# A one-column exp behind the last Silu of the seven-product stage

## The chip, the cores and the metric

The kernel runs on one core of a Trainium2 chip. The metric is the device time of one execution in microseconds (us). The core has five instruction streams that matter here: TensorE (PE, with its weight loads shown apart as PEld), VectorE (DVE), ScalarE (ACT), GpSimd (POOL) and the sync engine (SP), which only issues transfers (DMA). Each stream runs its own instructions in order and waits on semaphores for the others. ACT evaluates functions such as exp and Silu from a table that has to be loaded first: the program shows such a load as `ACT_TABLE_LOAD`, and the compiler puts one in wherever the next function is not in the table that stands loaded.

## The reference, cut to what matters

The reference is one layer of an encoder with two branches over 1024 positions and 16 learned leading ones:

```python
z = rms_norm(h, pre_w) @ w_in                       # one projection for everything
rq, rk, rv, rg, aq, ak, av, ag, gr, ga = split(z)
# branch A: bidirectional retention over chunks of 128, group norm, times silu(rg)
y_r = (norm(retention(rq, rk, rv)) * silu(rg)) @ w_rb
# branch B: attention in a window of +-128 with a sink logit per head
s = where(ok, (q @ k.T) * scale, -1e30)             # and 16 keys that are always seen
m = maximum(max(s), sink); p = exp(s - m)
p = p / (sum(p) + exp(sink - m))
y_a = (p @ v * silu(ag)) @ w_ab
out = h + rms_norm((sigmoid(gr) * y_r + sigmoid(ga) * y_a) @ w_o, post_w)
```

## The kernel before

All products are made in float32 from pairs of rounded halves: `mm3` (L92 to L97) issues three matmuls for each, high times high, low times high and high times low, and so L94, L95 and L96 carry nearly all of PE's time. The large projections are done by a scheme with seven block products in place of eight (`Phase`). The stage that the change speaks of is the first such phase, `first_phase`, which makes the gates `rg` (units 0 to 3, names that end in `y`) and the queries of the attention. Its epilogue for a gate tile is `z_post` (L1318): a multiply by the row norm on DVE (L1321), a Silu on ACT (L1331), a multiply by the retention's output on DVE (L1334), and a store (L1335). Behind it comes `attention()`.

The attention walks over 32 blocks of 64 queries by 4 heads. For a block, `stage1` makes the scores `ps` on PE, adds the mask and takes the row minimum `nm` on DVE (L1525, into one `raw` tile for each of two halves), takes exp on ACT (L1528, tile `p`, with the row sums `den`), the reciprocal of the sums on DVE (L1531) and the scaling of `p` on POOL (L1538). `stage2` transposes `p` on PE into `pt` (L1549, L1552) and splits it in halves on ACT (`pah`, `pbh`, L1555 and L1556) and DVE (`pal`, `pbl`, L110). `stage3` multiplies by the values (`vah`, `val`, and a small tile `v` for the edges) into `po`. Between these steps `fill` puts pieces of later projections (`pe`, whose copy out of PSUM is L886 and whose store is L887; `we` are their weights, loaded at L854 and summed on DVE at L861 to L863) as work for PE.

The order within each stream is set when the program is recorded, by a scheduler that orders instructions by a simulated timeline. `follow(...)` (L99) ties what is recorded inside it to come after given instructions; `marks(...)` looks the given names up in `last`, where lines such as L1528 (`last["exp"] = ...`) keep the newest instruction of a kind.

Transfers from SP go in turn over eight lanes, `DMAHW0` to `DMAHW7`: each waits until the one before it on its lane, eight rows ahead, has landed.

Of the kernel before, what the change touches and what calls it, by code (L numbers as in the profile page):

```python
# [7 lines left out]
F32 = mybir.dt.float32  # L8
R = mybir.dt.float32r
AF = mybir.ActivationFunctionType  # L10
# [6 lines left out]
P = 128  # L17
# [38 lines left out]
def block_kernel(ctx: ExitStack, tc: tile.TileContext, xT, x, meta, w_in, w_rb, w_ab, w_out, vecs, dec, sink,  # L56
                 post_w, rope, tab, out):
    nc = tc.nc
    PSUM = bass.MemoryType.PSUM

    keep = ctx.enter_context(tc.tile_pool(name="keep", bufs=1))
# [37 lines left out]
    def follow(*ins):  # L99

        st = ExitStack()
        for i in ins:
            st.enter_context(tc.issue_after(i))
        return st
# [11 lines left out]
    dtab = keep.tile([P, 28], F32, name="dtab")  # L116
    rcol = keep.tile([P, 9], F32, name="rcol")
    rbc = keep.tile([P, T], F32, name="rbc")
    rnw = keep.tile([P, KT], F32, name="rnw")
    mhalf = keep.tile([P, 16], F32, name="mhalf")  # L120
    nc.vector.memset(mhalf, -0.5)
# [802 lines left out]
    softmax, last = [], {}  # L924

    def marks(*names):
        return [last[m] for m in names if m in last]
# [383 lines left out]
    def z_fetch(u, i, j):  # L1311
        if u < 8:
            d = (oTr_d if u < 4 else oTa_d)[2 * (u % 4) + i, :, 512 * j:512 * j + 512]
            v = gtile(f"v{u}{i}{j}")
            nc.sync.dma_start(v, d)
            fetched[u, i, j] = v, d

    def z_post(u, i, j, o, to=None):  # L1318
        s = slice(512 * j, 512 * j + 512)
        to = o if to is None else to  # L1320
        nc.vector.tensor_tensor(to, o, rbc[:, half[j]], mul)  # L1321
        while late:
            late.pop()()
        if u >= 8:
            nc.scalar.activation(to, to, AF.Tanh, scale=0.5)
            nc.sync.dma_start(tg_d[2 * (u - 8) + i, :, s], to)
            return
        if u in (0, 1):
            z_fetch(u, i, j)
        v, d = fetched.pop((u, i, j))  # L1330
        nc.scalar.activation(to, to, AF.Silu)  # L1331

        def gated():
            nc.vector.tensor_tensor(to, to, v, mul)  # L1334
            nc.sync.dma_start(d, to)  # L1335
        late.append(gated)
# [118 lines left out]
    def first_post(u, i, j, o, to=None):  # L1455
        (query_post if u > 15 else z_post)(u - 16 * (u > 15), i, j, o, to)

    def first_fetch(u, i, j):
        if 1 < u < 16:
# [5 lines left out]
    first_seq[-14:] = [(u, p) for p in (1, 5, 6, 7, 4, 2, 3) for u in FIRST[-2:]]  # L1465
    first_phase = Phase("y", first_seq, w_loader(w_in, gates), first_post, first_fetch, paired=True)
    steps = run([(Phase("z", sequence(EARLY + LATER, (1, 3, 2, 5, 6, 7, 4)), pre_loader, z_post, z_fetch,
                        early=EARLY, pre=PRE),
                  act_src(oTr_d)),
# [260 lines left out]
        do(table, n)  # L1730
    zq_stack.close()
    gates_[0] = 6
    free[:] = ["pj"] * 3
    e_from[0] = pj
    a_stack = ExitStack()
# [147 lines left out]
```

## Time and profile before

| | us |
|---|---|
| three runs, median | 1052.22 |
| three runs, lowest and highest | 1050.63, 1053.98 |
| the profiled execution's own time | 1050.95 |
| its span in the trace | 1049.1 |
| PE busy in the span | 1029.7 |
| ACT busy in the span | 510.5 |

The profile shows one execution. Its times run from the start of the span; the 1.85 us between the span and the execution's own time lie around it. In the timeline a row gives the start, the duration, the engine, the line of the kernel, the operation, and out<-in; what stands in brackets is the idle time of the engine just before, and what ended it. `SPq` rows are transfers being issued, not their duration. In the chain of waits a DMA row runs from the issue to the landing.

### The profile page before, as it was taken

The page shows a single profiled execution, that of the slowest core. Times are in us where ns is not written, and L with a number is a line of the kernel's source. Part 1 is how long each engine was busy: PE and PEld are TensorE (multiplying, and loading weights), DVE is VectorE, ACT ScalarE, POOL GpSimd, SP SyncE. Part 2 cuts the span into 40 slices and gives each one's busy share as a digit, 9 for nine tenths or more (in the row PEclk, how much of TensorE's full clock was granted, in tenths as well). Part 3 has the DMA queues.
Part 4 walks back from the last instruction along what each step waited for, and adds up shares of the span by engine and source line. Part 5 has one row for each costly group of instructions (what it writes and reads, how often), then busy time and mean ns, then how long its engine had stood idle before and what let it go on. Part 6 is the DMA issues. An engine that isn't in the chain of part 4 may idle for free.

```text
span 1049.1 us, 17233 instructions
## 1 busy us (share of the span) xinstructions
PE 1029.7 (98%) x5797; PEld 892.3 (85%) x5797; DVE 841.5 (80%) x1734; ACT 510.5 (49%) x1116; POOL 216.5 (21%) x284
## 2 busy tenths in 40 slices
PE   9999999999999999999799999999999999999997
PEld 8998999989999888888689998888888888787885
DVE  7887788779899787985867886699899799767665
ACT  5541441423445643424567776476567354343443
POOL 3424235234232002231123331000000000111042
PEclk9999999999999999999899999999999999999999
DMA  9322311315244499998867784999899638789365
GB/s 340 157 81 91 102 42 51 112 38 194 78 145 139 137 413 311 264 308 217 310 212 218 240 250 154 359 383 337 307 301 334 233 130 276 195 243 305 94 101 81
DMA packets 117577, 217.17 MB, mean 207 GB/s; under 512 B 12672, under 2 KB 44320, under 8 KB 114864
## 3 DMA queue, kind: packets, MB, share of 16 engines
q1 hardware_dynamic: 110896, 204.52, 56.6%
q0 software_dynamic: 6304, 11.01, 7.3%
q8 instruction: 46, 0.75, 0.3%
q10 hardware_dynamic: 288, 0.53, 0.2%
q14 instruction: 43, 0.35, 0.1%
HBM read 142.57 MB, written 77.12 MB: 209 GB/s over the span
## 4 chain that ended last, share of the span: by engine, by line
PE 84%; DVE 6%; DMA 6%; issue 1%; POOL 1%; SPq 1%; ACT 1%; DVEq 0%; POOLq 0%; ACTq 0%
PE bz L95 5%; PE bz L94 5%; PE bz L96 5%; PE by L95 4%; PE by L94 4%; PE by L96 4%; PE pv L95 3%; PE pv L96 3%; PE pv L94 3%; PE bo L95 3%; PE bo L94 3%; PE br L95 2%; PE bo L96 2%; PE br L94 2%; PE br L96 2%; PE ba L95 2%
## 5 line engine op out<-in xcount | busy, mean ns | idle before, releaser
L94 PE MATMUL pv<-wh,big 128*128 128x256 f32 x256 | 73.3, 286 | 0.0
L95 PE MATMUL pv<-wh,big 128*128 128x256 f32 x256 | 72.9, 285 | 0.0
L96 PE MATMUL pv<-wl,big 128*128 128x256 f32 x256 | 72.5, 283 | 0.0
L1538 POOL TENSOR_SCALAR p<-p,den 128x352 f32<-128x352 f32 (+2 forms) x60 | 38.2, 650 | 125.6 <-DVE den L1531 100.3
L1369 POOL DMA_DIRECT2D mx_d<-c1a x4 | 3.5, 873 | 287.3 <-DVE c1a L1360 287.3
L94 PE MATMUL bz<-T,lhz 128*128 128x512 f32 x144 | 56.8, 395 | 0.0
L95 PE MATMUL bz<-T,llz 128*128 128x512 f32 x144 | 56.8, 394 | 0.0
L96 PE MATMUL bz<-T,lhz 128*128 128x512 f32 x144 | 56.8, 394 | 0.0
L1012 ACT CAST why<-wry 128x512 fp32r<-128x512 f32 x56 | 33.0, 620 | 46.3 <-PE by L96 27.4
L95 PE MATMUL by<-big,wly 128*128 128x512 f32 x128 | 50.7, 396 | 0.0
L94 PE MATMUL by<-big,why 128*128 128x512 f32 x128 | 50.4, 394 | 0.0
L96 PE MATMUL by<-big,why 128*128 128x512 f32 x128 | 50.3, 393 | 0.0
L1453 POOL DMA_DIRECT2D aq_d<-m_aq x32 | 27.3, 1282 | 104.7 <-DMA aq_d<-c1y 77.9
L95 PEld LDWEIGHTS pv<-wh,big 128*128 128x128 f32 x256 | 48.2, 188 | 0.3
L94 PEld LDWEIGHTS pv<-wh,big 128*128 128x128 f32 x256 | 48.2, 188 | 0.2
L96 PEld LDWEIGHTS pv<-wl,big 128*128 128x128 f32 x256 | 48.3, 189 | 0.2
L110 DVE TENSOR_TENSOR wly<-wry,why 128x512 fp32r<-128x512 f32 x56 | 37.8, 693 | 11.9 <-ACT why L1012 11.8
L1528 ACT ACTIVATE p<-raw,nm 128x353 f32<-128x353 f32 (+2 forms) x64 | 36.2, 567 | 18.3 <-DVE nm L1525 17.4
L595 ACT ACTIVATE op<-pa,rcol 128x256 f32<-128x256 f32 x32 | 15.2, 476 | 41.9 <-PE pa L96 41.6
L657 ACT ACTIVATE ost<-to,rnw 128x128 f32<-128x128 f32 x64 | 20.0, 365 | 31.4 <-PE to L652 21.8
L1525 DVE CUSTOM_DVE_ANT_0 raw<-ps,mask,nsink 128x352 f32<-128x352 f32 (+2 forms) x64 | 33.2, 548 | 2.4 <-ACT p L1528 1.9
L687 POOL TENSOR_TENSOR rs<-rs,mhalf 128x1 f32<-128x1 f32 x32 | 23.3, 727 | 52.6 <-DVE rs L686 49.3
(716 smaller groups left out, 3765.7 us busy)
## 6 DMA issues: line engine op xcount, KB each, us to landing
e<-e SPq DMA_DIRECT2D x60, 256.0 KB, 5.2
we<-in_w_in_dram SPq DMA_DIRECT2D x20, 512.0 KB, 5.6
wr<-in_w_in_dram SPq DMA_DIRECT2D x19, 512.0 KB, 4.2
wry<-in_w_in_dram SPq DMA_DIRECT2D x16, 512.0 KB, 7.0
tg<-tg_d SPq DMA_DIRECT2D x32, 256.0 KB, 4.9
T<-tT SPq DMA_DIRECT2D x6, 1024.0 KB, 10.2
T<-preT SPq DMA_DIRECT2D x6, 1024.0 KB, 8.1
wrz<-in_w_in_dram SPq DMA_DIRECT2D x20, 256.0 KB, 5.3
```

Source lines behind the costliest of these rows:

```text
L94: nc.tensor.matmul(o, ah, bh, start=first, stop=False, **kw)
L95: nc.tensor.matmul(o, al, bh, start=False, stop=False, **kw)
L96: latest[:] = [nc.tensor.matmul(o, ah, bl, start=False, stop=last, **kw).ins]
L110: return nc.vector.tensor_tensor(o, i, hi.bitcast(F32), ALU.subtract).ins
L595: nc.scalar.activation(o, pa[:, 0:256], AF.Copy, scale=rcol[:, c:c + 1])
L657: nc.scalar.activation(ost[0][:, e_, w0:w0 + P], to[:, P * e_:P * e_ + P], AF.Copy, scale=rnw[:, 2 * h + e_:2 * h + e_ + 1])
L687: nc.gpsimd.tensor_tensor(rs, rs, mhalf[:, 0:1], ALU.pow)
L1012: nc.scalar.copy(h, src)
L1453: nc.gpsimd.dma_start(d[a], m2[b], accum_op=ALU.add)
L1525: nc.vector.tensor_tensor_reduce(raw[e_][:, 1:1 + wid], s[:, 0:wid], mask[:, mo:mo + wid], -SCALE, nsink[:, hp:hp + 1], ALU.add, ALU.min, ...
L1528: last["exp"] = nc.scalar.activation(p[:, 0:1 + wid], raw[e_][:, 0:1 + wid], AF.Exp, scale=-1.0, bias=nm_[:, e_:e_ + 1], accum_out=den[:, ...
L1538: nc.gpsimd.tensor_scalar(pt[e_][:, 0:wid], pt[e_][:, 0:wid], den[:, e_:e_ + 1], 1.0, op0=ALU.mult, op1=ALU.mult)
```

## The change

A tile `warmed` of one float32 column is added to the pool `keep` (in SBUF, ahead of `rnw`; it takes 32 bytes of each partition, and every tile that is placed behind it moves up by 32 bytes). `z_post` keeps its newest Silu in `last["silu"]`. When all steps of the first phase have been recorded, and before the attention's pools are opened, an exp of a column of the constant tile `mhalf` into `warmed` is recorded behind the last Silu. Nothing reads `warmed`.

```diff
@@ -116,6 +116,7 @@
     rbc = keep.tile([P, T], F32, name="rbc")
+    warmed = keep.tile([P, 1], F32, name="warmed")
     rnw = keep.tile([P, KT], F32, name="rnw")
@@ -1328,7 +1329,7 @@
         v, d = fetched.pop((u, i, j))
-        nc.scalar.activation(to, to, AF.Silu)
+        last["silu"] = nc.scalar.activation(to, to, AF.Silu).ins
@@ -1730,6 +1731,8 @@
     zq_stack.close()
     gates_[0] = 6
+    with follow(*marks("silu")):
+        nc.scalar.activation(warmed, mhalf[:, 0:1], AF.Exp)
     free[:] = ["pj"] * 3
```

Lines of the changed kernel are one higher than before from L119 on and three higher behind the new lines L1734 and L1735, so the Silu of L1331 is L1332 there, the copy of L886 is L887, and the exp of L1528 is L1529.

On ACT, this stands at the end of the first phase and the start of the attention before:

```order
L1331 ACTIVATE c1y_6271<-c1y_6271 128x512
L1331 ACTIVATE u2y_6334<-u2y_6334 128x512
L1331 ACTIVATE u2y_6354<-u2y_6354 128x512
L886 COPY e_5_6655<-pe_5_6621 128x512
L886 COPY e_5_6682<-pe_5_6658 128x512
L1528 ACT_TABLE_LOAD
L1528 ACTIVATE p_0_6635,den_0_6629<-raw_6611,nm_0_6628 128x209
L1528 ACTIVATE p_0_6643,den_0_6629<-raw_6612,nm_0_6628 128x209
```

And this at the same place in the changed kernel:

```order
L1332 ACTIVATE c1y_6250<-c1y_6250 128x512
L1332 ACTIVATE u2y_6335<-u2y_6335 128x512
L1332 ACTIVATE u2y_6355<-u2y_6355 128x512
L1735 ACT_TABLE_LOAD
L1735 ACTIVATE warmed<-mhalf 128x1
L887 COPY e_5_6657<-pe_5_6623 128x512
L887 COPY e_5_6684<-pe_5_6660 128x512
L1529 ACTIVATE p_0_6637,den_0_6631<-raw_6613,nm_0_6630 128x209
L1529 ACTIVATE p_0_6645,den_0_6631<-raw_6614,nm_0_6630 128x209
```

The table load has moved from between the second copy of `e` and the first exp to between the last Silu and the first copy of `e`, the new exp stands behind it, and the two copies now stand behind both. The number of table loads is the same. Before, the load itself held a wait on lane `DMAHW4`; now the first exp holds it.

On SP, in both kernels alike, these transfers (with what each waits for) stand at the same place; the rows are those of before:

```order
L1335 DMA oTr_d<-u2y_6354 128x512 [waits DMAHW5_49,DVE_49]
L1613 DMA vah<-av_116 128x2048 [waits DMAHW6_49,PE_49]
L1614 DMA val<-av_117 128x2048 [waits DMAHW7_49,PE_49]
L1503 DMA v_0_6615<-av_116 64x128 [waits DMAHW0_49]
L1503 DMA v_0_6615<-av_117 64x128 [waits DMAHW1_49]
L1507 DMA v_0_6615<-vm_d 16x2x128 [waits DMAHW2_49]
L1507 DMA v_1_6619<-vm_d 16x2x128 [waits DMAHW3_49,DMASW7_49,DMASW6_49]
L887 DMA e_5_72<-e_5_6655 128x512 [waits DMAHW4_49,Activation_49]
L887 DMA e_5_75<-e_5_6682 128x512 [waits DMAHW5_49,Activation_49]
L864 DMA s_5_102<-we_1_6504 128x512 [waits DMAHW6_49,DVE_49]
L1503 DMA v_2_6747<-av_116 64x128 [waits DMAHW7_49]
```

Nothing moved here: the store `s_5` waits for lane 6, on which `vah` runs, and the row behind it, the load of the edge tile `v_2`, for lane 7, on which `val` runs. The rows of PE, DVE, POOL and SP are the same in both kernels throughout, apart from the line numbers and the numbers in the names.

## The prediction, made before the result was known

> **What bounds the kernel now.** I read the page first, for the bound, then who PE waits for, then the place of the change in the timeline, then the chain of waits behind it.
>
> ```profile
> span 1049.1 us, 17233 instructions
> PE 1029.7 (98%) x5797; PEld 892.3 (85%) x5797; DVE 841.5 (80%) x1734; ACT 510.5 (49%) x1116; POOL 216.5 (21%) x284
> PE 84%; DVE 6%; DMA 6%; issue 1%; POOL 1%; SPq 1%; ACT 1%; DVEq 0%; POOLq 0%; ACTq 0%
> ```
>
> PE is busy for 98% of the span, and ACT carries 1% of the chain that ended last. So ACT's time can only matter where PE stands idle. The view of PE's waits has eleven rows, 11.6 us in all; the longest and the last:
>
> ```profile
> PE pt L1549 <- POOL p L1538: 2.8, 2, 2.5
> PE ps L94 <- DVE nm L1525: 2.6, 1, 2.6
> PE pt L1549 <- DVE pal L110: 1.8, 2, 1.7
> ...
> PE pq L94 <- POOL w L107: 0.2, 1, 0.2
> ```
>
> The first three lie within 26 us of each other, where the attention begins, which is where the table load moves. The timeline there:
>
> ```profile
> 509.85 0.63 ACT L1331 ACTIVATE u2y<-u2y 128x512 f32<-128x512 f32 x1 [0.57 <-DVE u2y L1321]
> 510.39 0.57 ACT L886 COPY e<-pe 128x512 f32<-128x512 f32 x1
> 510.45 1.10 SPq L1335 DMA_DIRECT2D oTr_d<-u2y  x2
> 511.29 0.59 ACT L886 COPY e<-pe 128x512 f32<-128x512 f32 x1 [0.33 <-issue]
> 511.48 0.43 DVE L1525 CUSTOM_DVE_ANT_0 raw<-ps,mask,nsink 128x208 f32<-128x208 f32 x1
> 511.62 0.40 PE L94 MATMUL ps<-kTh,aqh 128*128 128x288 f32 x1 [2.58 <-DVE nm L1525]
> 511.65 0.41 SPq L1613 DMA_DIRECT2D vah<-av  x1
> 511.89 1.28 ACT L1528 ACT_TABLE_LOAD   x1
> 513.18 0.47 ACT L1528 ACTIVATE p<-raw,nm 128x209 f32<-128x209 f32 x1
> 513.78 0.52 DVE L1525 CUSTOM_DVE_ANT_0 raw<-ps,mask,nsink 128x288 f32<-128x288 f32 x1 [1.86 <-ACT p L1528]
> 515.39 0.47 PE L1549 MATMUL pt<-ident,p 128*128 128x128 f32 x1 [2.50 <-POOL p L1538]
> 515.68 0.53 SPq L887 DMA_DIRECT2D e<-e  x1
> ```
>
> The reader is to see that DVE has the first row minimum ready soon after 511.48, and the first exp starts only at 513.18, right behind the load. DVE then idles 1.86 us and PE 2.50 us behind that exp. So before, the load does stand in the way. But the chain of waits does not pass through it:
>
> ```profile
> 512.15 9.85 DMA val<-av
> 522.02 0.54 SPq L1503
> ...
> 526.41 0.58 SPq L733
> 527.04 5.71 DMA we<-in_w_in_dram
> 532.84 0.70 DVE we L861
> 533.57 0.69 DVE we L862
> 534.26 0.61 DVE pal L110
> 535.01 0.63 PE pt L1549 x4
> ```
>
> And the timeline of PE and DVE at its end:
>
> ```profile
> 532.84 0.69 DVE L861 TENSOR_TENSOR we<-we,we 128x512 f32<-128x512 f32 x1 [3.62 <-DMA we<-in_w_in_dram]
> 533.06 0.28 PE L96 MATMUL po<-pbl,v 80*128 80x256 f32 x1
> 535.01 0.63 PE L1549 MATMUL pt<-ident,p 128*128 128x128 f32 x4 [1.67 <-DVE pal L110]
> ```
>
> The load of `val` lands at 522.00. SP's next transfer waits for its lane, so SP stands until then; it issues without a gap from 522.02 to the `we` load at 527.04, which lands at 532.75; DVE, in order, does two sums before `pal`; and PE, out of work since about 533.34, starts again at 535.01. Every link of this runs from a transfer issued at 512.15.
>
> **The change part by part.** *The load and the exp beside it.* The last Silu ends at 510.48 (509.85 + 0.63). Two rows price what comes behind it, the load and the tiny exp at the program's start:
>
> ```profile
> L309 ACT ACT_TABLE_LOAD  x1: 1283/1283/1283, 1.6 to 1.6; - x1
> L309 ACT ACTIVATE warm<-warm x1: 203/203/203, 2.9 to 2.9; 128x1 f32<-128x1 f32 x1
> ```
>
> Load 510.48 to 511.77, new exp to 511.97; the first copy starts about 0.09 before the end of its forerunner, as 510.39 does against 510.48, so at 511.88; the second 0.50 later (0.59 less 0.09) at 512.38; the first real exp another 0.50 later at 512.88. Its inputs are there since about 511.6. That is 0.30 us earlier than 513.18, not 1.28: nearly all of the load still runs before the exp, since the two copies, which ran ahead of it before, now stand behind it. What is won is 0.40 between the copies' starts (0.90 before, 0.50 now) and 0.10 behind the second, whose full end the load had waited for; what is lost is the 0.20 of the new exp. Bounds: if the idle time between the copies is their own and comes again, the 0.40 goes and 0.10 us are lost; if the new exp overlaps wholly, 0.50 are won. I take 0.30, because PE had been done with all ahead of it at 509.04 (511.62 less 2.58), so the copies have nothing to wait for.
>
> From what the load takes: the Trainium skill, page "ScalarE: Activation LUTs", section "What ACT_TABLE_LOAD costs", puts a switch at about 2.66 us, with a drain of 1.38 behind a load of 1.28. By it the first exp would have begun at about 514.6, and it began at 513.18, 1.29 behind the load's start: the load's figure agrees with this trace, the drain does not show in it. The sum by that figure would be the same, since the load is moved and not removed.
>
> *The two copies of `e`* end 1.49 and 1.08 us later, at 512.45 and 512.97. Their stores are issued at 515.68 and behind, 2.7 us after, and PE's next product of this kind, which wants a bank, is later still:
>
> ```profile
> 516.69 0.78 PE L94 MATMUL pe<-big,w_4h 128*128 128x512 f32 x1
> ```
>
> So they cost nothing as long as the copies are not over 2.7 us later than reckoned.
>
> *What stands behind.* DVE's next `raw`, `den`, POOL's scaling and PE's transposes come 0.30 us earlier, and PE reaches its end of work near 533.04 instead of 533.34. What is late next is the `we` load. SP's rows do not move: the store of `u2y`, `vah` and `val` hang on Silu and DVE's product ahead of the moved load, `s_5` on lane 6, `v_2` on lane 7. So PE still starts at 535.01, and its wait there grows from 1.67 to 1.97. On the end: 0.00.
>
> *The 32 bytes.* All tiles behind `warmed` move. For the engines the nearest row is the exp itself, whose `p` tiles stand at six different places:
>
> ```profile
> L1528 ACT ACTIVATE p<-raw,nm x64: 454/588/596, 513.2 to 648.1; 128x353 f32<-128x353 f32 x48, 128x209 f32<-128x209 f32 x8, 128x289 f32<-128x289 f32 x8
> ```
>
> The longest is 596 and the median 588 ns over shapes up to 353 columns, so a place costs no engine 2%. For transfers no row here shows it. The two on the chain take 15.6 us together (9.85 and 5.71); at 5% either way that is 0.8 us there. I take 0, the exp's row being the nearest, and keep both ends.
>
> *Sum:* 0.30 us on ACT, 0 on the end. Against the profiled execution's own 1050.95 (span 1049.1 and 1.85 around it) the change gives 1050.95. That execution stands 1.3 below the median of 1052.22, which I therefore forecast unchanged: 1052.2.
>
> **The rivals.** *A: the 0.30 us pass through.* This needs the `we` load not to hold PE at 535.01. Against: DVE waited 3.62 us for it. It would give 1051.9; even the whole 1.28 of the load would give 1050.9. Both are within 0.3% (3.2 us, about what a measurement of this kernel can tell from no change).
>
> *B: the clock.* The view by windows, whose columns are PE, PEld, DVE, ACT and POOL busy, granted clock, DMA share and GB/s:
>
> ```profile
> 505.45:508.87 3.42, 3.42 (x16) 2.57 (x14) 3.42 (x7) 0.85 (x2) 0.00 (x0) 1.00 1.03 378
> 508.87:512.28 3.41, 0.83 (x6) 0.67 (x6) 2.95 (x8) 2.49 (x5) 0.00 (x0) 1.00 0.80 300
> 512.28:515.70 3.42, 0.92 (x6) 0.52 (x4) 1.92 (x7) 2.73 (x8) 1.20 (x2) 0.50 0.99 334
> 515.70:519.12 3.42, 3.15 (x11) 2.46 (x10) 2.68 (x7) 2.53 (x6) 1.94 (x3) 0.50 1.00 385
> 533.06:535.01 1.95, 0.28 (x4) 0.11 (x2) 1.92 (x4) 0.00 (x0) 0.00 (x0) 1.00 0.69 196
> 535.01:650.00 114.99, 114.70 (x739) 104.46 (x740) 90.83 (x241) 86.52 (x235) 31.82 (x50) 1.00 0.67 208
> ```
>
> After a stretch of 3.4 us in which PE was busy for 0.83, the clock was halved for 6.8 us. The wait of 1.67 at 535 left it at 1.00, one of 2.58 at 509 came before the halving; mine of 1.97 lies between. This is the slower rival: the time won in the first wait is put onto the second, and the clock falls there. It decides from the length of wait at which the clock falls. Behind 535.01 PE is busy for 114.70 of 114.99 us, so the loss is all on the path: one stretch of 3.42 at half speed costs 1.7 (1053.9), two, as seen here, 3.4 (1055.6). Against it: 0.3 us is little, and the stretch before the halving had PE busy for only 24%, where one of 3.4 us around a wait of 1.97 has 42%. The Trainium skill, page "TensorE: Matmul & The Clock Gate", section "The HAM clock gate", says the same of a window of about 3.4 us that runs freely and halves the clock after an idle one; the trace agrees in length and in the half. The reverse, that the earlier exp keeps the clock up at 512, saves about a microsecond of half-speed work and ends at the same 535.01.
>
> *C: the shift changes the transfers.* Transfers carry 6% of the chain, 63 us of 1049; at 5% that is 3.1 us, 1049.1 or 1055.3. For faster, it must take over 3.2 of the 11.6 us that PE waits in all, and of the three long waits only the 1.8 stands behind a transfer; so it is the less likely the larger it is. For slower there is no such bound.
>
> **How the numbers follow.** Forecast, nothing passes: 0.55. A: 0.07, inside 0.3%. B with one stretch: 0.05, inside; with two: 0.06, slower. C faster 0.14, C slower 0.13. So faster 0.14, within 0.67, slower 0.19. The forecast's own range is that of the three runs, 1050.6 to 1054.0. To leave out no more than 2 in 10 it has to reach into C and B, to about 1049.0 and 1055.3.
>
> **What would show it.** Right: the load at about 510.5, the first exp near 512.9, the transposes near 515.1, `val` still landing near 522, PE starting behind `we` near 535 with a wait near 2.0 and the clock at 1.00. Wrong: PE's start at 535 earlier or later by over a microsecond; the clock at half behind it; `val` or `we` landing otherwise; a new wait of PE elsewhere; or the first exp still at 513.2, which would say that the idle time between the copies was theirs.

## The result, and the profile after

The changed kernel took 1054.2 us (median of 13 runs, 1052.79 to 1058.0). The kernel before, run beside it on the same chip, took 1051.07 (13 runs, 1049.57 to 1054.26). The ratio is 1.003, with a 95% interval of 1.0019 to 1.0041: slower by 3.1 us, or by 2.0 to 4.3. Two executions of the runs below, one of 2056.0 us and one of 1696.16 us, are in the slow state, and medians and ratios leave them out.

The head of the changed kernel's page says where to look:

```profile
span 1051.7 us, 17234 instructions
PE 1031.8 (98%) x5797; PEld 892.9 (85%) x5797; DVE 841.3 (80%) x1734; ACT 511.2 (49%) x1117; POOL 219.4 (21%) x284
```

The span grew by 2.6 us (from 1049.1), and PE's busy time by 2.1 (from 1029.7), for the same 5797 matmuls. ACT has one instruction more and 0.7 us more work. PE's waits stayed what they were, 11.8 us in eleven rows against 11.6; the first three rows:

```profile
PE pt L1550 <- POOL p L1539: 2.7, 2, 2.4
PE ps L94 <- DVE nm L1526: 2.6, 1, 2.6
PE pt L1550 <- DVE pal L110: 1.6, 2, 1.4
```

So the time did not come from a wait. At the place of the change, the timeline of the changed kernel shows the load and the exp where they were put:

```profile
510.77 0.63 ACT L1332 ACTIVATE u2y<-u2y 128x512 f32<-128x512 f32 x1 [0.57 <-DVE u2y L1322]
511.42 1.28 ACT L1735 ACT_TABLE_LOAD   x1
512.54 0.40 PE L94 MATMUL ps<-kTh,aqh 128*128 128x288 f32 x1 [2.60 <-DVE nm L1526]
512.72 0.20 ACT L1735 ACTIVATE warmed<-mhalf 128x1 f32<-128x1 f32 x1
512.83 1.05 ACT L887 COPY e<-pe 128x512 f32<-128x512 f32 x2
513.77 0.48 ACT L1529 ACTIVATE p<-raw,nm 128x209 f32<-128x209 f32 x1
514.37 0.52 DVE L1526 CUSTOM_DVE_ANT_0 raw<-ps,mask,nsink 128x288 f32<-128x288 f32 x1 [1.54 <-ACT p L1529]
515.98 0.48 PE L1550 MATMUL pt<-ident,p 128*128 128x128 f32 x1 [2.38 <-POOL p L1539]
```

The last Silu already starts 0.92 us later than before (510.77 against 509.85), though nothing ahead of it in any stream was changed. Reckoned from that Silu, the first real exp starts 3.00 us behind it, where it was 3.33 before: 0.33 us are won here. The chain behind it is the one of before:

```profile
513.07 9.55 DMA val<-av
522.64 0.53 SPq L1504
...
527.64 5.87 DMA we<-in_w_in_dram
533.60 0.70 DVE we L862
...
535.02 0.61 DVE pal L110
535.77 0.63 PE pt L1550 x4
```

PE starts again at 535.77, against 535.01. The clock, the seventh figure of each row of the view by windows (behind the span of time, its length, and the busy times of PE, PEld, DVE, ACT and POOL), falls to half for 6.83 us, as before, but from 513.81 on where it was from 512.29 on (so the first row below is partly at full speed, 0.72, where it was 0.50). It stands at 1.00 behind the restart:

```profile
512.28:515.70 3.42, 1.06 (x6) 0.82 (x6) 1.88 (x9) 3.12 (x10) 0.61 (x1) 0.72 0.98 317
515.70:519.12 3.42, 2.87 (x9) 2.12 (x10) 2.94 (x8) 2.30 (x6) 2.53 (x4) 0.50 1.00 422
535.77:650.00 114.23, 113.80 (x732) 103.73 (x733) 89.95 (x240) 85.75 (x232) 31.80 (x50) 1.00 0.67 209
```

Where, then, do 2.6 us come from? PE's 5797 matmuls stand in the same order in both kernels, so each start can be subtracted from its counterpart:

| matmul | start before | start after | difference |
|---|---|---|---|
| `pq` L95 | 9.35 | 8.96 | -0.39 |
| `pv` L96 | 131.81 | 131.67 | -0.14 |
| `pb` L94 | 313.90 | 314.37 | +0.47 |
| `pt`, the restart | 535.01 | 535.77 | +0.76 |
| `bz` L94 | 653.37 | 654.62 | +1.25 |
| `bz` L95 | 795.70 | 797.69 | +1.99 |
| `br` L96 | 852.35 | 854.60 | +2.25 |
| `bo` L95 | 1024.09 | 1026.27 | +2.18 |

It is no step but a slope. From 653.37 to 852.35, where PE hardly waits, a full microsecond is added in 199 us. Matmuls that run back to back have moved apart. That shows in any stretch of one kind. Rows of PE's timeline in the middle of the `bz` products, of before:

```profile
699.94 0.40 PE L94 MATMUL bz<-T,lhz 128*128 128x512 f32 x1
...
702.72 0.40 PE L94 MATMUL bz<-T,lhz 128*128 128x512 f32 x1
```

and of after:

```profile
699.95 0.40 PE L94 MATMUL bz<-T,lhz 128*128 128x512 f32 x1
...
702.77 0.39 PE L94 MATMUL bz<-T,lhz 128*128 128x512 f32 x1
```

Each pair encloses twelve steps from matmul to matmul without a gap: 2.78 us before and 2.82 after, 232 and 235 ns a step. Over all products that stream `T` (the block sums of the later seven-product phases; `bz`, `br`, `ba` and `bo`, some 850 back-to-back steps) the mean step is 232.7 ns before and 234.7 after, which makes 1.7 us. Over all back-to-back matmuls of the kernel the steps add up to 2.62 us more, the whole growth of the span. The grouped lines show it as the mean of one matmul, in before and in after:

```profile
L96 PE MATMUL bz<-T,lhz 128*128 128x512 f32 x144 | 56.8, 394 | 0.0
```

```profile
L96 PE MATMUL bz<-T,lhz 128*128 128x512 f32 x144 | 57.1, 396 | 0.0
```

Their program, shape and order are the same in both. What differs is where `T` lies: 32 bytes higher.

### The profile page after: what moved, and what is told of

It reads as the page before. It is cut to its first block, busy times and chain, and to the rows that moved or that the text cites. A ratio compares the mean times of both kernels' runs of the same rounds, so it can differ in the third digit from the quotient of the medians.

```text
span 1051.7 us, 17234 instructions
## 1 busy us (share of the span) xinstructions
PE 1031.8 (98%) x5797; PEld 892.9 (85%) x5797; DVE 841.3 (80%) x1734; ACT 511.2 (49%) x1117; POOL 219.4 (21%) x284
## 4 chain that ended last, share of the span: by engine, by line
PE 46%; DMA 5%; DVE 2%; issue 1%; SPq 1%; ACT 1%; DVEq 0%; POOLq 0%; POOL 0%; ACTq 0%
PE bz L96 5%; PE bz L95 5%; PE bz L94 5%; PE bo L95 3%; PE bo L94 3%; PE bo L96 2%; PE br L96 2%; PE br L95 2%; PE br L94 2%; PE ba L95 2%; PE ba L96 2%; PE ba L94 2%; DMA we<-in_w_in_dram 1%; PE pe L94 1%; PE pe L95 1%; PE pe L96 1%
## 5 line engine op out<-in xcount | busy, mean ns | idle before, releaser
L94 PE MATMUL pv<-wh,big 128*128 128x256 f32 x256 | 73.5, 287 | 0.0
L95 PE MATMUL pv<-wh,big 128*128 128x256 f32 x256 | 73.1, 285 | 0.0
L96 PE MATMUL pv<-wl,big 128*128 128x256 f32 x256 | 72.5, 283 | 0.0
L96 PE MATMUL bz<-T,lhz 128*128 128x512 f32 x144 | 57.1, 396 | 0.0
L95 PE MATMUL bz<-T,llz 128*128 128x512 f32 x144 | 57.1, 396 | 0.0
L94 PE MATMUL bz<-T,lhz 128*128 128x512 f32 x144 | 57.1, 396 | 0.0
L96 PE MATMUL by<-big,why 128*128 128x512 f32 x128 | 50.6, 396 | 0.0
L95 PE MATMUL by<-big,wly 128*128 128x512 f32 x128 | 50.6, 395 | 0.0
L94 PE MATMUL by<-big,why 128*128 128x512 f32 x128 | 50.6, 395 | 0.0
L95 PEld LDWEIGHTS pv<-wh,big 128*128 128x128 f32 x256 | 48.3, 189 | 0.3
L94 PEld LDWEIGHTS pv<-wh,big 128*128 128x128 f32 x256 | 48.3, 189 | 0.2
L96 PEld LDWEIGHTS pv<-wl,big 128*128 128x128 f32 x256 | 48.3, 189 | 0.2
L1529 ACT ACTIVATE p<-raw,nm 128x353 f32<-128x353 f32 (+2 forms) x64 | 36.2, 567 | 17.8 <-DVE nm L1526 16.7
```

Source lines behind the costliest of these rows:

```text
L94: nc.tensor.matmul(o, ah, bh, start=first, stop=False, **kw)
L95: nc.tensor.matmul(o, al, bh, start=False, stop=False, **kw)
L96: latest[:] = [nc.tensor.matmul(o, ah, bl, start=False, stop=last, **kw).ins]
L1529: last["exp"] = nc.scalar.activation(p[:, 0:1 + wid], raw[e_][:, 0:1 + wid], AF.Exp, scale=-1.0, bias=nm_[:, e_:e_ + 1], accum_out=den[:, ...
```

## The experiments

In every run below the kernel computes the whole reference, and the streams of all engines hold the same instructions in the same order as before (with the load and the exp moved, where the text says so). Ratios are to the kernel before, run on the same chip; its medians beside the runs were 1051.26 (the first four), 1051.70 (the next four) and 1051.54 us (the last two). The ratios and their intervals are worked out from the single runs and are not the quotients of two medians; they differ from those by up to 0.0009.

**The shift alone.** The tile without the exp.

```diff
     rbc = keep.tile([P, T], F32, name="rbc")
+    warmed = keep.tile([P, 1], F32, name="warmed")
     rnw = keep.tile([P, KT], F32, name="rnw")
```

> The unused tile `warmed` of 32 bytes stays, the exp goes: every tile behind it stands 32 bytes higher, and all streams' rows are those of before. Theory 'placement' (the 32 bytes make PE's matmuls slower by a nanosecond or two each, all over the span): the same as the changed kernel, about 1054.2 us, ratio 1.003, and the matmuls of 512 columns that read `T` come 234 ns apart instead of 232. Theory 'exp' (the moved table load, the two late copies or the clock at 512 cost the time): as before, about 1051.1, ratio 1.000. Theory 'transfers' (the 32 bytes make transfers slower): about 1054 too, but with the time in PE's waits and not in its busy time.

Measured: 1053.16 us, ratio 1.0024 (1.0012 to 1.0035). The back-to-back steps of PE add up to 2.64 us more than before, against 2.62 with the whole change. The line of the `T` products:

```profile
L96 PE MATMUL bz<-T,lhz 128*128 128x512 f32 x144 | 57.1, 396 | 0.0
```

An unused tile of 32 bytes slows the kernel by nearly as much as the change does. The time is read from the twelve runs here and not from the profiled one, which was the fastest of them: its span is 1050.2 us, since the steps that are not back to back came out about 1.5 us shorter in it.

**The exp alone.** The exp writes a column of `sinkc`, a tile that is there already; no tile moves.

```diff
-        nc.scalar.activation(to, to, AF.Silu)
+        last["silu"] = nc.scalar.activation(to, to, AF.Silu).ins
...
+    with follow(*marks("silu")):
+        nc.scalar.activation(sinkc[:, 0:1], mhalf[:, 0:1], AF.Exp)
```

> The exp behind the last Silu stays but writes into a column of the tile `sinkc`, which nothing reads any more by then; no tile moves. Placement and transfers: as before, about 1051.1, ratio 1.000 (the prediction's own sum, 0.00 on the end), PE starting behind the `we` load near 535 with its wait grown by about 0.3. Exp: about 1054.2, ratio 1.003.

Measured: 1051.33 us, ratio 1.0003 (0.9991 to 1.0014), the steps of PE 0.13 us less. In the timeline of this kernel the last Silu starts at 509.80, 0.05 us from its place before, so the effect of the exp can be read by itself:

```profile
510.45 1.28 ACT L1734 ACT_TABLE_LOAD   x1
512.79 0.48 ACT L1528 ACTIVATE p<-raw,nm 128x209 f32<-128x209 f32 x1
```

and its chain of waits:

```profile
512.09 10.00 DMA val<-av
527.11 6.14 DMA we<-in_w_in_dram
...
535.51 0.63 PE pt L1549 x4
```

The first real exp starts at 512.79 instead of 513.18, and PE still waits for the `we` load: its restart is at 535.51, 0.50 later than before, by loads of `val` and `we` that took 10.00 and 6.14 us where they took 9.85 and 5.71. PE itself came later too. Its last product ahead of the restart starts at 533.98, 0.92 later than before, though its first transposes had started 0.38 earlier. In between lie the 6.83 us at half clock. They run from 514.79 here and from 512.29 before, and PE was busy for 6.34 us of them here and for 4.06 before; half of the difference, 1.1 us, is an estimate of what that cost. The wait for the loads took it up: it was 1.25 us, where it was 1.67. The exp is neither a gain nor a loss that this measurement can tell from none; one of a microsecond would not show in it.

**Larger shifts.** The unused tile with 16 and with 32 columns (64 and 128 bytes).

```diff
+    warmed = keep.tile([P, 16], F32, name="warmed")
```

> No exp, and an unused tile of 64 bytes in place of 32. Placement by the address modulo 64: all moved tiles stand as before in that measure, ratio 1.000. Placement by a coarser measure (128 or 256 bytes): some other ratio, 0.997 to 1.004. Exp: 1.000.

```diff
+    warmed = keep.tile([P, 32], F32, name="warmed")
```

> No exp, and an unused tile of 128 bytes. Placement by the address modulo 64 or 128: ratio 1.000. By 256 bytes or more, or by the distance to the tiles on the other side: some other ratio, 0.997 to 1.004. Exp: 1.000.

Measured: with 64 bytes 1052.11 us, ratio 1.001 (0.9996 to 1.0024); with 128 bytes 1048.08 us, ratio 0.9967 (0.9955 to 0.998). The time does not grow with the shift: four times the shift gains 3.2 us where the single one loses 2 to 3. At 64 bytes the steps of PE are 0.23 us longer in all, at 128 they are 4.35 us shorter. The `T` products at 128 bytes:

```profile
L96 PE MATMUL bz<-T,lhz 128*128 128x512 f32 x144 | 56.1, 389 | 0.0
```

and the same stretch of the timeline as above, 2.72 us for the twelve steps, 227 ns each:

```profile
699.96 0.39 PE L94 MATMUL bz<-T,lhz 128*128 128x512 f32 x1
...
702.68 0.39 PE L94 MATMUL bz<-T,lhz 128*128 128x512 f32 x1
```

**`T` alone.** Only the six `T` tiles, each of 4 x 512 columns, are moved, by an unused tile ahead of them in their own pool, of 8 columns and of 32.

```diff
     yp, gp, yt = (ctx.enter_context(tc.tile_pool(name=n, bufs=1, reuse_waits="tile")) for n in ("yp", "gp", "yt"))
+    yt.tile([P, 8], F32, name="ahead")
```

> No exp and no `warmed`; an unused tile of 32 bytes stands only ahead of the six `T` tiles (the moving operands of 864 of the matmuls of 512 columns behind 700 us). Placement, matmul by matmul: the `T` products come 1.8 to 2.2 ns further apart as in the run with the whole shift, 864 times, so about 1.7 us more, 1052.9, ratio 1.0016, and the products that read `big` stay as before. If the slowdown hangs on other tiles or on what DVE, ACT and the transfers do meanwhile: ratio 1.000.

```diff
+    yt.tile([P, 32], F32, name="ahead")
```

> The same with 128 bytes ahead of the `T` tiles and nothing else moved. Placement, matmul by matmul: 864 products 4.3 to 5.3 ns closer together, about 4.2 us less, 1047.0, ratio 0.996. If it hangs on other tiles: 1.000.

Measured: by 32 bytes 1052.69 us, ratio 1.001 (0.9997 to 1.0023); by 128 bytes 1048.34 us, ratio 0.9959 (0.9944 to 0.9974). Their lines:

```profile
L96 PE MATMUL bz<-T,lhz 128*128 128x512 f32 x144 | 57.0, 396 | 0.0
```

```profile
L96 PE MATMUL bz<-T,lhz 128*128 128x512 f32 x144 | 56.2, 390 | 0.0
```

By the times, the gain of 128 bytes is that of `T` alone; of the steps, 3.5 of the 4.35 us are. By 32 bytes the `T` products slow down as they did in the change, 234.3 ns a step, and all steps together are 1.33 us longer; by the times alone this run is within the measurement's reach of both no change and the whole of what was expected. The rest of the change's 2.62 us is spread over other products whose operands moved too, `by` with `big` first (about 0.35 us).

**Place or distance.** The weights of these products lie on the other side of SBUF, which the tile `warmed` does not move. So two things changed together: where `T` lies, and how far it lies from the weights. The first kernel moves the left side by 96 bytes; the second does so too and moves the right side, with the weights, down by 32.

```diff
+    warmed = keep.tile([P, 24], F32, name="warmed")
```

> No exp, an unused tile of 96 bytes in `keep`: the `T` rows stand at 192 modulo 256, the weights of their products (`lhz` and the like) stay at 224. It is one more point of the curve, with 96 (before), 128, 160 and 224 known as 232.4, 234.2, 233.4 and 227.6 ns: between 227.6 and 234, a ratio from 0.997 to 1.003.

```diff
+    over = ctx.enter_context(tc.tile_pool(name="over", bufs=1, side="right"))
+    over.tile([P, 8], F32, name="over")
...
+    warmed = keep.tile([P, 24], F32, name="warmed")
```

> As the run with 96 bytes, but the tiles of the other side, the weights among them, are moved down by 32 bytes, to 192 modulo 256. If the distance of the moving rows to the weights decides, `T` and weights stand alike again as with 128 bytes, and the `T` products come 227.6 ns apart. If the place of the moving rows alone decides, they come as far apart as in the run with 96 bytes alone.

Measured: 1052.57 us, ratio 1.0001 (0.9989 to 1.0014), and 1048.65 us, ratio 0.9963 (0.9947 to 0.998). The lines of the first and of the second (whose line numbers are two higher):

```profile
L96 PE MATMUL bz<-T,lhz 128*128 128x512 f32 x144 | 57.0, 396 | 0.0
```

```profile
L98 PE MATMUL bz<-T,lhz 128*128 128x512 f32 x144 | 56.1, 389 | 0.0
```

`T` lies at the same bytes in both. With the weights at their old place its products are slow, and with the weights 32 bytes lower they are fast. The time of the first does not show all of this: its back-to-back steps are some 1.9 us longer than before, and its ratio allows 1.5 us at most. In its profiled execution the other steps are 2.1 us shorter; why is not shown.

**The wide tile in the changed kernel, and the weights alone.** Two runs close the circle: the change with `warmed` 32 columns wide, and a kernel in which `T` and all of the left side stay and the right side moves down by 32 bytes.

```diff
+    warmed = keep.tile([P, 32], F32, name="warmed")
...
+        nc.scalar.activation(warmed[:, 0:1], mhalf[:, 0:1], AF.Exp)
```

> The changed kernel with its load and exp as they are, and the tile `warmed` 128 bytes wide in place of 32 (the exp writes its first column). If the shift of the tiles is the whole cause and the exp costs nothing, this must come out as the 128-byte shift without the exp did: 1048.1 us, ratio to before 0.997, and the 512-column products of `T` at a mean of 389 to 390 ns (394 before, 396 with the change as it was). If the exp or the moved load had a part in the loss of 3.1 us that the shifts hid, it stays above that by the part: at 1049.5 or more.

```diff
+    over = ctx.enter_context(tc.tile_pool(name="over", bufs=1, side="right"))
+    over.tile([P, 8], F32, name="over")
```

> No exp and no tile among those of the left side: an unused tile of 32 bytes on the right side of SBUF, which moves the weights of the `T` products down by 32 bytes and leaves the tiles of `T` where they stood. Theory (the distance between the moving rows and the weights decides, modulo 256 bytes): it is the same distance as in the changed kernel, so the products of `T` come to a mean of 396 ns, and the time rises by some 1.5 to 3 us, to 1052.9 to 1054.4, ratio 1.0015 to 1.003. Rival (the place of `T` alone decides): `T` stays at 394 to 395 ns and the time is that of before, 1.000.

Measured: 1049.11 us, ratio 0.9978 (0.9963 to 0.9993), and 1053.8 us, ratio 1.0024 (1.001 to 1.0039). Their lines:

```profile
L96 PE MATMUL bz<-T,lhz 128*128 128x512 f32 x144 | 56.1, 389 | 0.0
```

```profile
L98 PE MATMUL bz<-T,lhz 128*128 128x512 f32 x144 | 57.1, 396 | 0.0
```

Without an exp and without a shift of `T`, the weights' move alone gives the loss of the change, with the steps of PE longer by 2.62 us, as there. The change with a wide tile is faster than before; its 1049.11 stands between the 1048.1 of the same shift without the exp and the 1049.5 set as the mark for a part of the exp. The two intervals overlap (0.9955 to 0.998 and 0.9963 to 0.9993), spans are 1046.9 in both, and the steps of PE are shorter by 4.42 and 4.35 us, so no part of the exp is seen, while one of about a microsecond is not ruled out by these two alone. One thing in the profiled execution of the wide tile is what rival B described. PE's wait ahead of the restart was 2.43 us there, and the clock was halved for one stretch behind it:

```profile
534.89 0.63 PE L1550 MATMUL pt<-ident,p 128*128 128x128 f32 x4 [2.43 <-DVE pal L110]
532.13:535.55 3.42, 0.99 (x10) 0.82 (x9) 2.79 (x5) 0.00 (x0) 0.00 (x0) 1.00 0.78 241
535.55:538.96 3.41, 3.41 (x11) 2.83 (x10) 2.81 (x8) 3.25 (x9) 0.42 (x1) 0.50 0.70 195
```

The restart came 0.11 us earlier than before, and 3.5 us on PE was 1.44 us behind. `T` by 32 bytes, which has no exp, shows the same elsewhere: a wait of 2.64 us up to 620.68, and half clock from 621.04 for 3.41 us. So this is not a mark of the exp, and how often it comes up in either kernel cannot be told from one profiled execution of each.

All runs together, ordered by the distance from the weights to `T` in bytes, modulo 256 (worked out from where the tiles lie in each program: the `T` tiles start at 96 before, those weights at 224, 96 - 224 = -128):

| distance, bytes | mean step of the `T` products, ns | runs, with their ratios |
|---|---|---|
| 128 | 232.7, 232.7 | before; exp alone 1.0003 |
| 160 | 234.7, 234.5, 234.6, 234.3 | the change 1.003; shift alone 1.0024; weights alone 1.0024; `T` by 32 1.001 |
| 192 | 233.7 | shift by 64 1.001 |
| 224 | 233.6 | shift by 96 1.0001 |
| 0 | 227.9, 227.8, 227.8, 229.0 | shift by 128 0.9967; left 96, right 32 0.9963; the change with a wide tile 0.9978; `T` by 128 0.9959 |

Every way to reach a distance gives its step within 0.4 ns, but for the 229.0 of the last, for which no run here shows a reason. Runs that beat both kernels are those with the distance 0; the simplest, the unused 128 bytes ahead of `T`, is at 0.9959.

The products that stream `big` stand at several distances within one kernel, and so they test this inside single traces (steps between 512-column matmuls, without those over 250 ns; by this count `T` is at 232.3 before and 234.3 after). Before, the steps of `big` take 230.8 ns at distance 0 and 232.6 at each of 64, 128 and 192, some 400 steps at each; modulo 512, they take 230.8 at 0 and 230.8 at 256. After, `big` stands at 32, 96, 160 and 224 and takes 232.7, 232.3, 231.7 and 233.8. So distance 0 is the fast one here too. At 160, however, `big` is at 231.7 where `T` is at 234.3: something besides the distance counts.

## Why the prediction was wrong

*The load and the exp beside it*: right. The load took 1.28 us directly behind the Silu, the exp 0.20, the two copies together 1.05, and the first real exp, reckoned from the last Silu, came 0.33 us (in the change) and 0.34 us (exp alone) earlier, for the 0.30 of the sum. The drain of 1.38 us that the Trainium skill, page "ScalarE: Activation LUTs", section "What ACT_TABLE_LOAD costs", puts behind a load shows here no more than before: `warmed` starts at 512.72, 0.02 us behind the load's end.

*The copies of `e`*: right; no wait for them came up.

*What stands behind*: right that the exp comes earlier and that PE restarts behind the `we` load, wrong on the way between. DVE's wait behind the exp fell from 1.86 to 1.54 and PE's from 2.50 to 2.38. But PE did not come to its end of work 0.30 us earlier. It came 1.0 us later in the changed kernel and 0.92 later with the exp alone, so the wait there was not 1.97 but 1.41 and 1.25. With the exp alone most of this is the half clock, which fell later and on more work; the prediction had taken an earlier exp to save half-speed work, if anything. In the changed kernel 0.92 us of it had been lost ahead of the last Silu. And with the exp alone the gain of 0.38 at the first transposes (515.01 against 515.39) has become a loss of 0.50 at the restart, by the two loads.

*The 32 bytes*: this is the step that failed. It took the exp's 454 to 596 ns over six places as the nearest row and said that a place costs no engine 2%, and from that took 0. Three things were wrong with it. The row was of ACT, and what moved with the tile was the distance between two operands of PE. It mixed three widths, so that its longest and its median say little of a place: the 48 exps of 353 columns alone take 574 to 596 ns, a spread of nearly 4%. And the bound was far too coarse: PE is busy for 1029.7 us, so 2% of it would be 20 us, and the 0.9% that the `T` products got slower (2.0 of 232.7 ns) already makes 1.7. The term measured +2.6 us, all of it in the steps between PE's matmuls; the tile alone gave 1.0024, or 2.5 us.

*Rival A* did not show: the restart came 0.76 us later in the changed kernel and 0.50 later with the exp alone, and 0.11 earlier with the wide tile. *Rival B* did not come in the changed kernel, where the clock stood at 1.00 behind the restart, nor with the exp alone. It did come in the profiled execution of the changed kernel with the wide tile, at about its price for one stretch (1.55 us between the restart and 3.5 us behind it, for 1.7). *Rival C* had the right cause, the shift, and the wrong resource: it was priced by the transfers on the chain, and those took 9.55 and 5.87 us, 0.30 less and 0.16 more than before. By its own rule (for slower there is no bound from PE's waits) it stood on the right side.

That the wider range, up to 1055.3, holds the measured 1054.2 is luck: its upper end was worked out from B's two stretches at half clock and C's slower transfers, and neither made this result.

The first lead in the trace lay ahead of the change: the Silu was 0.92 us late before any changed instruction had run.

## What to carry to other kernels

A new tile is a change to every tile placed behind it. Where TensorE is busy for 98% of the span, ask first which of its operands move against each other, and price a place from rows of that engine: 2.6 us in 1049, or 0.25%, spread over the steps of its matmuls, was all of this result. Where a kernel ends slower by some tenths of a per cent and no wait has grown, subtract the start times of the same matmuls: a slope says spacing, a step says a wait; and run the tile without the work, and the work without the tile.

## What the runs showed of the hardware

The step between back-to-back matmuls of 128x512 that stream `T` was 227.8 to 234.7 ns at full clock, a spread of 3%, and it went with the distance in SBUF between the streamed operand and the weights: shortest where both start at the same byte modulo 256, longest 160 bytes apart. For the products that stream `big` distance 0 was the shortest too (230.8 ns against 232.6 before), but 224 the longest (233.8 after), so the curve is not the same for all products. `T` alone could not tell a period of 256 from a longer one; `big` was as fast at 256 as at 0 modulo 512 (230.8 ns both), which fits 256. In the timeline of before, the weight load of the next product runs beside the streaming of the present one:

```profile
700.64 0.39 PE L94 MATMUL bz<-T,lhz 128*128 128x512 f32 x1
700.64 0.19 PEld L95 LDWEIGHTS bz<-T,llz 128*128 128x128 f32 x1
```

That the two reads get in each other's way is the plain reading of a cost that goes by their distance; no run here shows it directly, and it stays open. The Trainium skill, page "TensorE: Matmul & The Clock Gate", section "Step-by-step: what each phase is for", says that loading the next tile's weights takes no read bandwidth from the running matmul. If that holds and nothing else ties the two reads together, the distance should not matter; here it did, by up to 6.9 ns a matmul, and the measurement decides for this kernel.

In each of the twelve traces the clock was halved once between 511 and 516, for one, two or three times 3.41 us. Behind PE's wait at the restart, between 534 and 537, it stayed at 1.00 after the eleven waits of 0.65 to 1.81 us, and was halved for 3.41 us after the one of 2.43.
